# Weight totals of a seven-product matrix multiplication: prepared in DRAM for three FFN stages, with three products and the first tiles reordered

## The chip, the cores and the metric

The kernel runs on one core of a Trainium2 chip, in one launch. The metric is the device time of that launch in microseconds (us). Before the change it took 2440.33 us (median of three runs, 2434.14 to 2443.38). One further execution was recorded by the hardware profiler. The engines are named as in its profile: PE (TensorE, the matrix engine), PEld (its weight loads), DVE (VectorE), ACT (ScalarE), POOL (GpSimd) and SP (the engine whose queue issues most DMAs).

## The reference, cut to what matters

```python
def reference(x, ...):                    # x: (1, 512, 1024), two layers
    for l in range(2):
        h = rms_norm(x, norm_g[l, 0])
        x = x + 0.5 * swiglu(h, ffn_w_gate[l, 0], ffn_w_up[l, 0], ffn_w_down[l, 0])
        ...                               # three attention branches, gates, W_o: the "mixer"
        h = rms_norm(x, norm_g[l, 2])
        x = x + 0.5 * swiglu(h, ffn_w_gate[l, 1], ffn_w_up[l, 1], ffn_w_down[l, 1])
    return rms_norm(x, final_g)

def swiglu(h, w_gate, w_up, w_down):      # 1024 x 2816, 1024 x 2816, 2816 x 1024
    return (jax.nn.silu(h @ w_gate) * (h @ w_up)) @ w_down
```

All is float32. The kernel gets that precision by splitting each operand into a high part (a cast) and a low part (the remainder), and adding high x high, high x low and low x high.

## The kernel before

The program is a chain of stages: FFN (0,0), mixer 0, FFN (0,1), FFN (1,0), mixer 1, FFN (1,1), with (layer, place) as the code counts them. An FFN has a gate-up part and a down part. The 2816 hidden features are 22 tiles of 128. The first two tiles of a gate-up part (four in stage (0,0)) are plain: 24 matmuls of 512 columns for the gate, 24 for the up half. Every later tile is done by `Seven.tile` (L535), which replaces eight block products by seven, with sums of blocks as operands. Stages (0,1), (1,0) and (1,1) are called ready stages, since a part of their weight sums lies prepared.

A tile's weights are four blocks of 128 x 512 side by side, two of the gate (A11, A12) and two of the up weight (A21, A22). A tile needs:
- `wa`: the gate tile as it is, for products 1 and 2. It is loaded to `raw` (L494).
- `w31`: the gate tile and the up tile added in a certain way, for products 5 and 7. It is `wsum`, loaded ready from the DRAM tile `d_s` in ready stages (L434); in stage (0,0) the sum is made by an accumulating DMA (L438).
- `w24`: two further totals, made in place in `raw` by `others` (L502) once `wa` has been parted: the first half of `raw` gets the second half of `wsum` added, then the second half gets the first half added. In ready stages two accumulating DMAs of POOL do that (L507). In stage (0,0), and for the first tile of every stage, two additions of DVE do it (L509). They serve products 6 and 3.
- `w22`: A22 alone, for product 4, loaded to `a22` (L500).

`parted` (L99) casts a tile to its high half on ACT (L102) and subtracts on DVE (L103). `raw` has three buffers, `wsum` two, the halves four.

The matmuls of a tile stand on PE in the order 1, 5, 4 of the tile before, 6, 2, 3, 7. Products 1, 6, 7 and 4 gather in one PSUM bank (`mm` in the rows), 5 and 3 in another (`pr`), 2 in a third (`pv`). Product 6 may start only when ACT has copied product 1 out of the shared bank (L580). Each product has four matmuls with the high half of the weights and then four with the low half. In ready stages products 2 to 7 are "wide": one matmul takes 512 columns, the high and the low half of the other operand at once. The low half of the weights meets 256 columns (L523). In stage (0,0) only products 3, 4 and 5 are wide.

`in_order` fixes the order of a tile's instructions on each engine to the order of the code; the engines are otherwise coupled by semaphores. In a tile, ACT and DVE do this, in order: sum of product 7, `wa` of the next tile (with the two POOL DMAs behind it), `w24` of this tile, the copies of products 1 and 5, `w22`, the copy of 6, and `w31` of the next tile. In the first tile `sides.last()` (L602) also makes the fourth operand side.

`prepare` (L441) is a generator whose steps make the `d_s` tiles: a step copies 512 KB from DRAM to DRAM on SP's queue (L454) and lets POOL add the up tile to an earlier copy (L449). `weights` (L82), which loads every plain weight tile, advances it, by a rate held in `owed`. This happens in the mixers alone: in mixer 0 for two stages, at 48 steps on 72 weight loads, and in mixer 1 for one, at 24 on 72.

`position_tables` and `small_values` (L213, L253) make small tables for the attention. They stand ahead of tile 8 of stage (0,0) (L297).

Of the kernel before, what the change touches and what calls it, by code (L numbers as in the profile page):

```python
# [16 lines left out]
P = 128  # L17
# [14 lines left out]
GBUFS = 2 * MF  # L32
WIDE, WIDE_FIRST = frozenset((2, 3, 4, 5, 6, 7)), frozenset((3, 4, 5))
# [3 lines left out]
def encoder(ctx: ExitStack, tc: tile.TileContext, a: dict, out: bass.AP):  # L37
# [42 lines left out]
    prepared, ahead, owed = {}, [], [0.0, 0.0]  # L80

    def weights(src, width=1024):  # L82
        raw = wpool.tile([P, 1024], F32, tag="raw", name="raw", bufs=3)
        hi = wpool.tile([P, 1024], F32R, tag="whi", name="whi")
        lo = wpool.tile([P, 1024], F32R, tag="wlo", name="wlo")
        for c in range(0, src.shape[-1], width):
            w = slice(c, min(c + width, src.shape[-1]))
            loaded[:] = [nc.sync.dma_start(raw[:, w], src[:, w]).ins]
            nc.scalar.copy(hi[:, w], raw[:, w])  # L89
            lower[:] = [nc.vector.tensor_tensor(out=lo[:, w], in0=raw[:, w], in1=f(hi[:, w]), op=ALU.subtract).ins]  # L90
        owed[0] += owed[1]
        while ahead and owed[0] >= 1:
            owed[0] -= 1
            with tc.issue_after(loaded[0]):
                if next(ahead[0], ahead) is ahead:
                    ahead.pop(0)
        return hi, lo
# [115 lines left out]
    def position_tables(fp):  # L213


        parts = fp.tile([64, 36], F32R, tag="g", name="parts", bufs=GBUFS)
        nc.scalar.copy(parts, tab)
        nc.vector.tensor_tensor(out=parts[32:64], in0=tab[32:64], in1=f(parts[32:64]), op=ALU.subtract)
        for i in range(2):
            ps = st_tile()  # L220
            nc.tensor.matmul(ps[0:36, :], parts, hot[i], start=True, stop=True)
# [60 lines left out]
    def ffn(l, i, h, nxt=None):  # L282

        with tc.tile_pool(name="ffn", bufs=1) as fp, ExitStack() as order:
# [3 lines left out]
            if first:  # L288
                xs, sides, ps = opening(l, i, h, fp, ghi, glo)
                order.enter_context(tc.issue_after(h.squared))  # L290
            else:
                sides = []
            loads = []
            start, plain = (2, 4) if first else (0, 2)
            for m in range(start, MF):
                if m >= plain:
                    if first and m == plain + 4:  # L297
                        with tiles.in_order():
                            position_tables(fp)
                            small_values(fp)  # L300
                    if m == plain:
# [124 lines left out]
    def added(l, i, m, fp, load=None):  # L426

        gu = a["w_gu"][l, i, m]
        with ExitStack() as order:
# [3 lines left out]
            if (l, i) in prepared:  # L433
                loaded[:] = [nc.sync.dma_start(t, prepared[l, i][m]).ins]  # L434
                return t.rearrange("p n c -> p (n c)")
# [5 lines left out]
    def prepare(l, i):  # L441


        prepared[l, i] = {}
        waiting = []

        def accumulate():
            t, src = waiting.pop(0)
            nc.gpsimd.dma_start(t.rearrange("p n c -> p (n c)"), src, accum_op=ALU.add, max_dma_last_dim=4096)  # L449

        for m in range(2, MF):
            gu = a["w_gu"][l, i, m]
            t = prepared[l, i][m] = dram.tile([P, 2, S], F32, tag=f"d_s{l}{i}_{m}", name="d_s")
            nc.sync.dma_start(t, gu.rearrange("n p c -> p n c")[:, :, 0:S])  # L454
            waiting.append((t, gu[1]))
            if len(waiting) > 2:
                accumulate()
            yield
        while waiting:
            accumulate()  # L460
            yield

    class Seven:


        def __init__(self, l, i, h, fp, sides, ghi, glo):
# [3 lines left out]
            self.raw, self.sums, self.a22, self.wa, self.w31 = {}, {}, {}, {}, {}  # L470
# [16 lines left out]
        def fetch(self, m, sums=None):  # L487

            if m >= MF:
                return  # L490
            (l, i), fp = self.at, self.fp
            self.sums[m] = sums or added(l, i, m, fp)
            self.raw[m] = wpool.tile([P, 1024], F32, tag="raw", name="raw", bufs=3)
            nc.sync.dma_start(self.raw[m], a["w_gu"][l, i, m, 0])  # L494
# [7 lines left out]
        def others(self, m, engine):  # L502

            s2, s4 = self.raw[m][:, :S], self.raw[m][:, S:]
            for out, more in ((s2, self.sums[m][:, S:]), (s4, s2)):
                if engine is nc.gpsimd:
                    engine.dma_start(out, more, accum_op=ALU.add)  # L507
                else:
                    engine.tensor_tensor(out=out, in0=more, in1=out, op=ALU.add)  # L509

        def product(self, n, bank, w, b, start=False, stop=False):


            (wh, wl), ps = w, bank[:, 0]
            for k, bk in enumerate(b):
                go = start and k == 0
                if n in self.wide:
                    nc.tensor.matmul(bank, wh[k], bk, start=go, stop=False, skip_group_check=True)  # L518
                else:
                    nc.tensor.matmul(ps, wh[k], bk[:, 0], start=go, stop=False, skip_group_check=True)  # L520
                    nc.tensor.matmul(ps, wh[k], bk[:, 1], start=False, stop=False, skip_group_check=True)  # L521
            for k, bk in enumerate(b):
                nc.tensor.matmul(ps, wl[k], bk[:, 0], start=False, stop=stop and k == 3, skip_group_check=True)  # L523
# [11 lines left out]
        def tile(self, m):  # L535
# [29 lines left out]
            with self.in_order():  # L565
                self.fetch(m + 2)
                self.fetch_a22(m + 1)
                self.product(1, one, blocks(wa), [s.b11 for s in sides], start=True)
                rest()
                if not last:  # L570
                    self.wa[m + 1] = room()
                    parted(self.raw[m + 1], self.wa[m + 1])
                    if self.ready:
                        self.others(m + 1, nc.gpsimd)
                if first:
                    self.others(m, nc.vector)
                parted(self.raw.pop(m), w24)
# [22 lines left out]
                if first:  # L600
                    for s in sides:
                        s.last()  # L602
                if not last and not self.ready:
                    self.others(m + 1, nc.vector)
# [12 lines left out]
                self.product(7, one, blocks(w31), side(3))  # L617
            u3 = self.halves(1, 6, 7)
# [706 lines left out]
    h = Norm(0, gain(0, 0))  # L1325
    for l in range(DEPTH):
# [103 lines left out]
```

## Time and profile before

| | |
|---|---|
| time, median of 3 runs | 2440.33 us (2434.14 to 2443.38) |
| profiled execution, its own time | 2435.98 us |
| its span | 2433.8 us, so 2.2 us lie around it |
| gate-up part with seven products, one tile in the steady state | 9.86 us |
| DMA traffic | 388.37 MB, mean 160 GB/s |
| DVE / ACT / POOL busy | 1713.3 / 1323.3 / 362.4 us |

How to read it: a busy engine is one that executes an instruction. The matmuls are pipelined and their ends are modelled, so what PE loses is read from its idle time and from the distance of the starts. An entry such as "[2.79 <-ACT gu L580]" says that the engine was idle for 2.79 us ahead of the row and that the end of ACT's instruction at L580 released it. "PEclk" is the share of the clock that TensorE was granted.

### The profile page before, as it was taken

The page shows a single profiled execution, that of the slowest core. Times are in us where ns is not written, and L with a number is a line of the kernel's source. Part 1 is how long each engine was busy: PE and PEld are TensorE (multiplying, and loading weights), DVE is VectorE, ACT ScalarE, POOL GpSimd, SP SyncE. Part 2 cuts the span into 40 slices and gives each one's busy share as a digit, 9 for nine tenths or more (in the row PEclk, how much of TensorE's full clock was granted, in tenths as well). Part 3 has the DMA queues.
Part 4 walks back from the last instruction along what each step waited for, and adds up shares of the span by engine and source line. Part 5 has one row for each costly group of instructions (what it writes and reads, how often), then busy time and mean ns, then how long its engine had stood idle before and what let it go on. Part 6 is the DMA issues. An engine that isn't in the chain of part 4 may idle for free.

```text
span 2433.8 us, 34871 instructions
## 1 busy us (share of the span) xinstructions
PE 2401.1 (99%) x12762; PEld 2056.0 (84%) x12762; DVE 1713.3 (70%) x3067; ACT 1323.3 (54%) x2433; POOL 362.4 (15%) x518
## 2 busy tenths in 40 slices
PE   9999999999999999999999999999999999999998
PEld 7899888888888888888888888888888888888887
DVE  7899345766666689993499983467666666998822
ACT  6566225756566456663256652367566564565631
POOL 3100013322100111110011110133110000111100
PEclk9999999999999999999999999999999999999999
DMA  6566368774776346664356654566544433565632
GB/s 198 155 188 176 122 183 229 201 198 124 200 185 182 132 137 184 186 176 135 113 155 185 184 158 131 165 185 154 151 132 130 141 112 123 160 183 156 182 121 69
DMA packets 138347, 388.37 MB, mean 160 GB/s; under 512 B 16248, under 2 KB 21672, under 8 KB 138176
## 3 DMA queue, kind: packets, MB, share of 16 engines
q1 hardware_dynamic: 97536, 278.50, 34.2%
q0 software_dynamic: 39488, 105.79, 21.7%
q8 instruction: 100, 1.64, 0.3%
q10 hardware_dynamic: 1152, 1.86, 0.2%
q14 instruction: 71, 0.58, 0.1%
HBM read 334.15 MB, written 75.53 MB: 168 GB/s over the span
## 4 chain that ended last, share of the span: by engine, by line
PE 92%; DVE 2%; DMA 2%; ACT 2%; issue 1%; POOL 0%; SPq 0%; POOLq 0%; ACTq 0%; DVEq 0%
PE mm L117 8%; PE mm L116 8%; PE mm L119 8%; PE mm L518 7%; PE mm L523 6%; PE pr L518 6%; PE mm L364 5%; PE mm L363 5%; PE mm L366 5%; PE pr L523 3%; PE pv L518 2%; PE mm L520 2%; PE mm L521 2%; PE mm L1214 2%; PE mm L1210 2%; PE mm L1209 2%
## 5 line engine op out<-in xcount | busy, mean ns | idle before, releaser
L89 ACT CAST whi<-raw 128x1024 fp32r<-128x1024 f32 (+1 forms) x258 | 265.6, 1032 | 401.8 <-PE mm L364 185.0
L90 DVE TENSOR_TENSOR wlo<-raw,whi 128x1024 fp32r<-128x1024 f32 (+1 forms) x258 | 313.7, 1216 | 227.8 <-ACT whi L89 108.5
L116 PE MATMUL mm<-h,whi 128*128 128x512 f32 x800 | 318.4, 398 | 0.0
L117 PE MATMUL mm<-h,whi 128*128 128x512 f32 x800 | 313.7, 392 | 0.0
L364 PE MATMUL mm<-g,whi 128*128 128x512 f32 x528 | 205.5, 389 | 0.0
L363 PE MATMUL mm<-g,whi 128*128 128x512 f32 x528 | 205.5, 389 | 0.0
L119 PE MATMUL mm<-h,wlo 128*128 128x512 f32 x800 | 197.7, 389 | 0.0
L103 DVE TENSOR_TENSOR wlo<-raw,whi 128x1024 fp32r<-128x1024 f32 x156 | 184.9, 1219 | 15.3 <-ACT whi L102 15.1
L119 PEld LDWEIGHTS mm<-h,wlo 128*128 128x128 f32 x800 | 150.2, 188 | 31.3
L102 ACT CAST whi<-raw 128x1024 fp32r<-128x1024 f32 x156 | 158.2, 1052 | 32.5 <-DMA raw<-raw 14.5
L117 PEld LDWEIGHTS mm<-h,whi 128*128 128x128 f32 x800 | 150.5, 188 | 29.0 <-DVE h L148 0.5
L116 PEld LDWEIGHTS mm<-h,whi 128*128 128x128 f32 x800 | 150.4, 188 | 29.0 <-ACT h L147 0.6
L366 PE MATMUL mm<-g,wlo 128*128 128x512 f32 x528 | 131.4, 389 | 0.0
L955 ACT ACTIVATE lg<-lg,negm 128x256 f32<-128x256 f32 (+1 forms) x192 | 114.2, 595 | 26.8 <-DVE negm L952 25.5
L625 ACT COPY gu<-mm 128x512 f32<-128x512 f32 (+1 forms) x78 | 42.0, 538 | 159.1 <-PE mm L523 154.6
L449 POOL DMA_DIRECT2D d_s<-in_w_gu x60 | 51.4, 857 | 474.3 <-DMA d_s<-in_w_gu 415.5
L366 PEld LDWEIGHTS mm<-g,wlo 128*128 128x128 f32 x528 | 99.1, 188 | 20.6
L363 PEld LDWEIGHTS mm<-g,whi 128*128 128x128 f32 x528 | 99.2, 188 | 20.4
L364 PEld LDWEIGHTS mm<-g,whi 128*128 128x128 f32 x528 | 99.1, 188 | 20.4
L556 DVE TENSOR_TENSOR gu<-pr,gu 128x256 f32<-128x256 f32 x234 | 98.1, 419 | 3.6 <-ACT gu L586 1.1
L507 POOL DMA_DIRECT2D raw<-wsum x57 | 49.7, 872 | 322.3 <-DVE wlo L103 289.6
L103 DVE TENSOR_TENSOR wlo<-wsum,whi 128x1024 fp32r<-128x1024 f32 x78 | 94.7, 1215 | 0.0
(326 smaller groups left out, 6011.5 us busy)
## 6 DMA issues: line engine op xcount, KB each, us to landing
raw<-in_w_gu SPq DMA_DIRECT2D x94, 512.0 KB, 4.5
d_s<-in_w_gu SPq DMA_DIRECT2D x60, 512.0 KB, 5.4
d_s<-in_w_gu POOLq DMA_DIRECT2D x60, 512.0 KB, 6.5
wsum<-d_s SPq DMA_DIRECT2D x60, 512.0 KB, 3.6
raw<-in_w_down SPq DMA_DIRECT2D x48, 512.0 KB, 3.6
raw<-in_w_gate SPq DMA_DIRECT2D x48, 512.0 KB, 4.2
raw<-in_w_qk SPq DMA_DIRECT2D x44, 512.0 KB, 3.8
a<-in_w_gu SPq DMA_DIRECT2D x78, 256.0 KB, 4.7
```

The source lines that it names most:

```text
L89: nc.scalar.copy(hi[:, w], raw[:, w])
L90: lower[:] = [nc.vector.tensor_tensor(out=lo[:, w], in0=raw[:, w], in1=f(hi[:, w]), op=ALU.subtract).ins]
L102: nc.scalar.copy(hi, src)
L103: nc.vector.tensor_tensor(out=lo, in0=src, in1=f(hi), op=ALU.subtract)
L116: nc.tensor.matmul(ps, wh, xhi[k], start=k == 0, stop=False)
L117: nc.tensor.matmul(ps, wh, xlo[k], start=False, stop=False)
L119: nc.tensor.matmul(ps, wl, xhi[k], start=False, stop=k == n - 1)
L363: nc.tensor.matmul(ps, w[k][0], ghi[c + k], start=c + k == 0, stop=False)
L364: nc.tensor.matmul(ps, w[k][0], glo[c + k], start=False, stop=False)
L366: nc.tensor.matmul(ps, w[k][1], ghi[c + k], start=False, stop=c + k == MF - 1)
L518: nc.tensor.matmul(bank, wh[k], bk, start=go, stop=False, skip_group_check=True)
L523: nc.tensor.matmul(ps, wl[k], bk[:, 0], start=False, stop=stop and k == 3, skip_group_check=True)
```

## The change

Four things change.

1. `prepare` makes two DRAM tiles for each weight tile: `d_odd` (what `d_s` was) and `d_even` (the two `w24` totals). One step holds two copies on SP's queue and up to three accumulating DMAs on POOL, each two steps behind the one that it needs. The steps are spread over more stages by the table `PACE`: the down parts of (0,0), (0,1) and (1,0), both mixers, and the seven-product tiles of (0,1). `drained` runs what is left when a stage begins.
2. In ready stages `d_even` is loaded to a `raw` buffer of its own, and neither POOL's two DMAs nor, in the first tile, DVE's two additions are there any more. SP's order is now `a22`, `wsum`, `raw`, `even`.
3. In the first tile of each stage, `wa` of the next tile is parted after the copy of product 6 rather than ahead of `w24`. The tables of stage (0,0) are cut in two: the operands and the small values stand ahead of tile 8, the matmuls and what follows them ahead of tile 9.
4. In products 2, 4 and 7 the four matmuls with the low half of the weights come first.

```diff
+PACE = {"mixer": (0.36, 0.3), "seven": {(0, 1): 0.4}, "down": {(0, 0): 0.3, (0, 1): 0.4, (1, 0): 0.25}}
+LOW_FIRST = (2, 4, 7)
...
-        owed[0] += owed[1]
-        while ahead and owed[0] >= 1:
...
+        ahead_by(owed[1])
...
         nc.vector.tensor_tensor(out=parts[32:64], in0=tab[32:64], in1=f(parts[32:64]), op=ALU.subtract)
+        yield
         for i in range(2):
...
+            drained(l, i)
+            owed[1] = 0
...
                     if first and m == plain + 4:
+                        tables = position_tables(fp)
                         with tiles.in_order():
-                            position_tables(fp)
+                            next(tables)
                             small_values(fp)
+                    if first and m == plain + 5:
+                        with tiles.in_order():
+                            list(tables)
...
+            owed[1] = PACE["down"].get((l, i), 0)
             for m in range(KC):
...
+        for k in range(2, MF + 6):
+            if k < MF:
...
+                tiles[k] = t31, t24
+                nc.sync.dma_start(t31, gu.rearrange("n p c -> p n c")[:, :, 0:S])
+                nc.sync.dma_start(flat(t24), gu[0])
+            if k - 2 in tiles:
+                accumulate(flat(tiles[k - 2][0]), a["w_gu"][l, i, k - 2, 1])
+            if k - 4 in tiles:
+                t31, t24 = tiles[k - 4]
+                accumulate(t24[:, 0], t31[:, 1])
+            if k - 6 in tiles:
+                t24 = tiles[k - 6][1]
+                accumulate(t24[:, 1], t24[:, 0])
             yield
...
+    def ahead_by(n):
+
+        owed[0] += n
+        while ahead and owed[0] >= 1:
+            owed[0] -= 1
+            with tc.issue_after(loaded[0]):
+                if next(ahead[0], ahead) is ahead:
...
+    def drained(l, i):
+
+        while (l, i) in due:
+            if next(ahead[0], ahead) is ahead:
...
+            self.raw[m] = raw(a["w_gu"][l, i, m, 0])
+            if self.ready:
+                self.even[m] = raw(prepared[l, i][m][1].rearrange("p n c -> p (n c)"))
...
-                if engine is nc.gpsimd:
-                    engine.dma_start(out, more, accum_op=ALU.add)
-                else:
-                    engine.tensor_tensor(out=out, in0=more, in1=out, op=ALU.add)
+                nc.vector.tensor_tensor(out=out, in0=more, in1=out, op=ALU.add)
+            self.even[m] = self.raw[m]
...
+            if n in LOW_FIRST:
+                low(False)
+                high(True)
+            else:
+                high(False)
+                low(True)
...
+            with self.in_order():
+                self.fetch_a22(m + 1)
+                self.fetch(m + 2)
+                self.product(1, one, blocks(wa), [s.b11 for s in sides], start=True)
+                rest()
+                if not first:
+                    next_wa()
+                elif not self.ready:
+                    self.others(m)
+                parted(self.even.pop(m), w24)
...
                 if first:
+                    next_wa()
                     for s in sides:
                         s.last()
...
+            ahead_by(PACE["seven"].get(self.at, 0))
...
+    due[:] = [(0, 1), (1, 0), (1, 1)]
+    ahead[:] = [prepare(*at) for at in due]
     for l in range(DEPTH):
...
-        ahead[:] = [prepare(*at) for at in ([(0, 1), (1, 0)] if l == 0 else [(1, 1)])]
-        owed[:] = 0.0, 24 * len(ahead) / 72
+        owed[1] = PACE["mixer"][l]
         mixer(l, n1, n2)
-        for steps in ahead:
-            for _ in steps:
-                pass
-        ahead.clear()
+        owed[1] = 0
```

What this moves on the engines is shown at three places. The first is DVE at the end of the plain tiles and in the first seven-product tile of stage (0,1). `wlo<-wsum` is the low half of `w31`, `wlo<-raw` of `wa` or `w24`, L384 and L128 finish the plain tile. Before:

```order
L103 TENSOR_TENSOR wlo<-wsum,whi 128x1024
L103 TENSOR_TENSOR wlo<-raw,whi 128x1024
L384 TENSOR_TENSOR gu<-pg,gu 128x512
L384 TENSOR_TENSOR gu<-mm,gu 128x512
L509 TENSOR_TENSOR raw<-wsum,raw 128x512
L128 TENSOR_TENSOR g<-gu,g 128x512
L509 TENSOR_TENSOR raw<-raw 128x512
L128 TENSOR_TENSOR g<-gu,g 128x512
L103 TENSOR_TENSOR wlo<-raw,whi 128x1024
L556 TENSOR_TENSOR gu<-pr,gu 128x256
L593 TENSOR_TENSOR w22l<-a_8861,w22h 128x512
L556 TENSOR_TENSOR gu<-gu 128x256
```

The same place with the change:

```order
L100 TENSOR_TENSOR wlo<-wsum,whi 128x1024
L100 TENSOR_TENSOR wlo<-raw,whi 128x1024
L389 TENSOR_TENSOR gu<-pg,gu 128x512
L389 TENSOR_TENSOR gu<-mm,gu 128x512
L125 TENSOR_TENSOR g<-gu,g 128x512 x2
L607 TENSOR_TENSOR gu<-pr,gu 128x256
L647 TENSOR_TENSOR w22l<-a_8913,w22h 128x512
L607 TENSOR_TENSOR gu<-gu 128x256
L100 TENSOR_TENSOR wlo<-raw,whi 128x1024
```

The two additions (L509) are gone, the early `wlo<-raw` is now `w24` of this tile, and the late one, now last, is `wa` of the next tile.

The second place is SP's queue in the seven-product tiles of stage (0,1), two tiles' worth. `a` is `a22`. Before:

```order
L434 DMA wsum<-d_s 128x1024
L494 DMA raw<-in_w_gu 128x1024
L500 DMA a_8983<-in_w_gu 128x512
L434 DMA wsum<-d_s 128x1024
L494 DMA raw<-in_w_gu 128x1024
L500 DMA a_9092<-in_w_gu 128x512
```

With the change:

```order
L439 DMA wsum<-d_odd 128x1024
L526 DMA raw<-in_w_gu 128x1024
L526 DMA raw<-d_even 128x1024
L538 DMA a_9147<-in_w_gu 128x512
L439 DMA wsum<-d_odd 128x1024
L465 DMA d_odd<-in_w_gu 256x1x512
L466 DMA d_even<-in_w_gu 16x8192
L526 DMA raw<-in_w_gu 128x1024
L526 DMA raw<-d_even 128x1024
L538 DMA a_9263<-in_w_gu 128x512
```

A tile loads `d_even` as well, and in eight of the twenty tiles of this stage the two copies of a step stand between the load of `wsum` and that of `raw`.

The third place is PE in a ready stage, products 2 and 3. Before:

```order
L518 MATMUL pv<-h_8497,whi 128x512
L518 MATMUL pv<-h_8539,whi 128x512
L518 MATMUL pv<-h_8581,whi 128x512
L518 MATMUL pv<-h_8623,whi 128x512
L523 MATMUL pv<-h_8497,wlo 128x256
L523 MATMUL pv<-h_8539,wlo 128x256
L523 MATMUL pv<-h_8581,wlo 128x256
L523 MATMUL pv<-h_8623,wlo 128x256
L518 MATMUL pr<-h_8497,whi 128x512
L518 MATMUL pr<-h_8539,whi 128x512
```

With the change:

```order
L555 MATMUL pv<-h_8541,wlo 128x256
L555 MATMUL pv<-h_8589,wlo 128x256
L555 MATMUL pv<-h_8631,wlo 128x256
L555 MATMUL pv<-h_8673,wlo 128x256
L555 MATMUL pv<-h_8541,whi 128x512
L555 MATMUL pv<-h_8589,whi 128x512
L555 MATMUL pv<-h_8631,whi 128x512
L555 MATMUL pv<-h_8673,whi 128x512
L555 MATMUL pr<-h_8541,whi 128x512
L555 MATMUL pr<-h_8589,whi 128x512
```

The same matmuls are there; eight wide ones now stand in a row where four did, and likewise eight narrow ones.

More of the change, by code (lines that the diff above doesn't have):

```diff
@@ L469, in __init__ @@
             self.wide = WIDE if self.ready else WIDE_FIRST
-            self.raw, self.sums, self.a22, self.wa, self.w31 = {}, {}, {}, {}, {}
+            self.raw, self.even, self.sums, self.a22, self.wa, self.w31 = {}, {}, {}, {}, {}, {}
             self.tail, self.behind = (), {}
@@ L500, in fetch_a22, with others, mm, high @@
                 nc.sync.dma_start(self.a22[m], a["w_gu"][self.at + (m, 1)][:, S:])
-        def others(self, m, engine):
+        def others(self, m):
             s2, s4 = self.raw[m][:, :S], self.raw[m][:, S:]
             for out, more in ((s2, self.sums[m][:, S:]), (s4, s2)):
-                if engine is nc.gpsimd:
-                    engine.dma_start(out, more, accum_op=ALU.add)
-                else:
-                    engine.tensor_tensor(out=out, in0=more, in1=out, op=ALU.add)
+                nc.vector.tensor_tensor(out=out, in0=more, in1=out, op=ALU.add)
+            self.even[m] = self.raw[m]
         def product(self, n, bank, w, b, start=False, stop=False):
[L514 to L523, printed above, removed]
+            (wh, wl), ps, count = w, bank[:, 0], [0]
+            def mm(out, wk, bk, last):
+                count[0] += 1
+                go, end = start and count[0] == 1, stop and last
+                nc.tensor.matmul(out, wk, bk, start=go, stop=end, skip_group_check=True)
+            def high(end):
+                for k, bk in enumerate(b):
+                    if n in self.wide:
+                        mm(bank, wh[k], bk, end and k == 3)
+                    else:
+                        mm(ps, wh[k], bk[:, 0], False)
+                        mm(ps, wh[k], bk[:, 1], end and k == 3)
+            def low(end):
+                for k, bk in enumerate(b):
+                    mm(ps, wl[k], bk[:, 0], end and k == 3)
+            if n in LOW_FIRST:
+                low(False)
+                high(True)
+            else:
+                high(False)
+                low(True)
         def halves(self, *n):
@@ L564, in tile, with next_wa @@
             w24 = room()
[L565 to L569, printed above, removed]
+            def next_wa():
                 if not last:
@@ L572, in tile @@
                     parted(self.raw[m + 1], self.wa[m + 1])
[L573 to L577, printed above, removed]
+            with self.in_order():
[8 more added lines that the diff above has]
+                parted(self.even.pop(m), w24)
                 rest()
```

43 lines of the change are left out of this document (20 added, 23 removed).

## The prediction

> **What bounds the kernel now.** First the page's busy times, then PE's waits, then the stages.
>
> ```profile
> span 2433.8 us, 34871 instructions
> PE 2401.1 (99%) x12762; PEld 2056.0 (84%) x12762; DVE 1713.3 (70%) x3067; ACT 1323.3 (54%) x2433; POOL 362.4 (15%) x518
> ...
> PE mm L518 <- ACT gu L580: 12.8, 8, 3.0
> PE mm L520 <- ACT gu L580: 2.4, 1, 2.4
> ```
>
> PE is busy for 2401.1 of 2433.8 us. The change takes no matmul away, so it can win only idle PE time and time at a lower clock. The waits view (engine and line, what it waited for, total us, count, longest) has one wait that matters: product 6 waits until ACT has copied product 1 (L580), 15.2 us in nine places. Windows by stage (length, busy times, then granted clock, DMA share, GB/s) show where:
>
> ```profile
> 364.00:832.00 468.00, 465.04 (x2404) 391.27 (x2403) 316.63 (x660) 285.93 (x599) 93.28 (x140) 1.00 0.68 182
> 876.00:1090.00 214.00, 210.98 (x1257) 186.52 (x1255) 202.97 (x352) 137.10 (x233) 34.87 (x40) 1.00 0.64 177
> 1566.00:2032.00 466.00, 464.78 (x2408) 391.96 (x2409) 311.98 (x661) 285.94 (x599) 84.58 (x122) 1.00 0.51 141
> 2090.00:2310.00 220.00, 213.16 (x1253) 188.26 (x1252) 198.86 (x337) 138.78 (x232) 34.24 (x40) 0.98 0.64 176
> ```
>
> The first and third are mixers 0 and 1, the others the gate-up parts of (0,1) and (1,1). In these DVE is nearly as full as PE (202.97 of 214), which matters below. A stall of PE costs more than itself. Narrow windows behind three stalls give the clock (before the last two numbers):
>
> ```profile
> 1244.20:1250.90 6.70, 5.79 (x18) 4.92 (x19) 4.18 (x9) 4.41 (x10) 0.87 (x1) 0.52 0.90 249
> 2210.20:2213.50 3.30, 3.30 (x12) 2.77 (x11) 2.66 (x6) 1.50 (x3) 0.87 (x1) 0.53 0.33 58
> 2234.10:2237.40 3.30, 3.30 (x12) 2.76 (x11) 2.63 (x6) 1.52 (x3) 0.87 (x1) 0.53 0.28 49
> ```
>
> Half the clock for 6.7, 3.3 and 3.3 us loses 3.4 + 1.7 + 1.7 = 6.8 us. The Trainium skill, TensorE: Matmul & The Clock Gate, section "Why this matters for your kernels", says that gaps up to about 3 us are safe. Here idle times of 2.42 to 2.96 us (rows below) stand right ahead of the drops, so by this trace they belong to the stalls; by the rule they would not, which is rival C.
>
> **The totals loaded instead of added by POOL.** In the steady state of a ready stage the rows are these (start, length, engine):
>
> ```profile
> 1344.66 2.35 DVE L103 TENSOR_TENSOR wlo<-raw,whi 128x1024 fp32r<-128x1024 f32 x2
> 1346.28 0.86 POOL L507 DMA_DIRECT2D raw<-wsum  x1 [5.24 <-DVE wlo L103]
> 1350.57 0.89 POOL L507 DMA_DIRECT2D raw<-raw  x1 [3.42 <-DMA raw<-wsum]
> 1353.23 2.00 ACT L102 CAST whi<-raw 128x1024 fp32r<-128x1024 f32 x2
> 1355.66 0.36 ACT L580 COPY gu<-mm 128x256 f32<-128x256 f32 x1
> 1356.79 1.09 PE L518 MATMUL mm<-pair,whi 128*128 128x512 f32 x4
> ...
> DMA to landing us min/median/max: 3.2/3.4/6.1
> ...
> DMA to landing us min/median/max: 4.1/4.5/7.1
> ```
>
> The subtraction of the next `wa` (the first of the two at 1344.66) releases POOL, whose two DMAs run one behind the other, at 3.4 us median each (of the landing rows the first is L507's, the second that of L494's loads of `raw`). The second lands at 1350.57 + 3.4 = 1354.0, and ACT's second cast (1353.23 + 1.0) needs it at 1354.2. Slack 0.2 us, and 0.8 more until product 6, which starts 1356.79 - 1356.02 behind the copy. A landing of 6.1 breaks that, as here in stage (1,1):
>
> ```profile
> 2201.63 0.86 POOL L507 DMA_DIRECT2D raw<-raw  x1 [4.63 <-DMA raw<-wsum]
> 2207.70 1.04 ACT L102 CAST whi<-raw 128x1024 fp32r<-128x1024 f32 x1 [3.58 <-DMA raw<-raw]
> 2209.59 1.42 PE L518 MATMUL mm<-pair,whi 128*128 128x512 f32 x4 [2.79 <-ACT gu L580]
> 2233.50 1.45 PE L518 MATMUL mm<-pair,whi 128*128 128x512 f32 x4 [2.42 <-ACT gu L580]
> ```
>
> With the change `raw` of tile m+2 takes the buffer of `even` of tile m. Its load waits for the end of the pair of subtractions (1344.66 + 2.35 = 1347.0), lands 4.5 later at 1351.5, and is cast at 1353.2: slack 1.7 plus 0.8, with one DMA in place of two. `even` itself has a whole tile more. So the mid-stage stalls should go. Their sum is 12.8 us less the three at first tiles (5.4, below), 7.4, and two of the clock windows, 3.4: **-10.8**.
>
> What one copy of a step takes, by the page's list of issues (size, median us to landing):
>
> ```profile
> d_s<-in_w_gu SPq DMA_DIRECT2D x60, 512.0 KB, 5.4
> ```
>
> Stage (0,1) pays for it, since eight steps of preparation run in its tiles. Mixer 0 has 24 more steps than mixer 1 and a DMA share of 0.68 against 0.51; 0.17 x 467 us / 24 = 3.3 us of all DMA engines for an old step, and about 6.6 for a new one, which moves twice as much. At 0.4 steps a tile the share there goes from 0.64 towards 0.9 (0.4 x 6.6 / 9.86 = 0.27, with 9.86 us a tile). The copies stand ahead of `raw` on SP's queue. No row shows a step beside such a tile: by the median landing it costs nothing, by the longest `raw` landing in the rows, 7.1, it is 7.1 - 4.5 - 2.5 = 0.1 late, and should both copies (5.4 for one) queue ahead of it, some 3 us. I take 0.25 us for each of the eight, **+2**, nearer to the first two, with 0 and +38 (rival A) as ends.
>
> **The first tile of the ready stages.** Stage (1,0), with what PE and ACT waited for:
>
> ```profile
> 1241.52 0.63 PE L523 MATMUL pr<-pair,wlo 128*128 128x256 f32 x4
> 1242.98 0.68 DVE L509 TENSOR_TENSOR raw<-raw 128x512 f32<-128x512 f32 x1
> 1243.75 1.04 ACT L102 CAST whi<-raw 128x1024 fp32r<-128x1024 f32 x1 [2.97 <-DVE raw L509]
> 1245.12 2.08 PE L518 MATMUL mm<-pair,whi 128*128 128x512 f32 x4 [2.96 <-ACT gu L580]
> ...
> 899.17 1.20 PE L518 MATMUL mm<-pair,whi 128*128 128x512 f32 x4 [1.23 <-ACT gu L580]
> ```
>
> DVE's additions (L509) hold ACT's cast of `w24`, which holds the copy of product 1. With `even` loaded and parted early, product 6 can start when product 5 ends. That removes 2.96, 1.23 in (0,1) and about as much in (1,1), 5.4 together, and the clock window of 3.4. What is late next is DVE: `wa` of tile 3 is now subtracted behind `w22` and the copy of 6, and the four subtractions of `sides.last()` come behind it. I count on in DVE's new order from 1241.2 (three instructions of 512 columns, 0.6 each, ahead of the row at 1242.98), with 1.13 for a subtraction of 1024 columns (half of 2.35, less the overlap), 0.6 for 512, 0.4 for 256, and ACT's casts where they come later. DVE then ends `w24` of the second tile at about 1254.0. That tile starts at 1241.5 + 0.5 + 4 x 1.4 = 1247.6 and its product 6 needs the low half 5.2 later (4.3 for products 1, 5 and 4, 0.9 for its high half), at 1252.8. So a new wait of about 1.2 us in each of three stages; a wait of that size did not lower the clock at 899 (four wide matmuls in 1.20, against 2.08 at 1245). Together -5.4 - 3.4 + 3.6 = **-5.2**; the ends are -8.8 with no new wait, and -2 with one of 2.3.
>
> **The tables in (0,0).**
>
> ```profile
> 91.19 0.64 PE L523 MATMUL mm<-side,wlo 128*128 128x256 f32 x4
> 93.81 0.83 PE L221 MATMUL st<-hot,parts 64*36 64x512 f32 x2 [1.97 <-DVE parts L218]
> 96.02 0.18 DVE L257 TENSOR_SCALAR bg<-bg 128x24 f32<-128x24 f32 x1
> 98.29 0.20 ACT L265 ACTIVATE ls<-ls 128x2 f32<-128x2 f32 x1 [1.21 <-DVE ls L264]
> 102.50 0.35 ACT L580 COPY gu<-mm 128x256 f32<-128x256 f32 x1
> 102.90 0.39 PE L520 MATMUL mm<-pair,whi 128*128 128x256 f32 x1 [2.44 <-ACT gu L580]
> ```
>
> PE's own wait (1.97) goes, but ACT is what is late: the second exponential (98.29) waits for a DVE chain (from L257 on), ahead of which the table work takes 2.2 us (from the operands' end at 93.8 to 96.0). That moves behind, so the copy and product 6 come about 2.3 earlier; PE, being earlier by more, waits longer there (about 4.6). The table matmuls (0.8) move to the next tile. Net -1.5, less a longer clock window after the longer wait: **-1**, with -3 and +3 as ends.
>
> **The mixers.** Mixer 0 idles PE for 468 - 465.0 = 3.0 us, mixer 1, at half the steps, for 466 - 464.8 = 1.2; POOL's accumulations wait for copies, and the attention's POOL work waits behind them. At 0.36 steps a load mixer 0 becomes like mixer 1: **-1.5**, with -3 and +2 as ends, since a step now has three POOL DMAs. Mixer 1 keeps its rate (0.3 against 0.33). In the down parts three buffers are loaded ahead, each worth 24 matmuls of 0.227 (1.81 / 8, below), 5.4 us; that covers a copy's 5.4, and if it did not, each of some 23 steps there could cost up to 1 us.
>
> **Low halves first.** It makes eight wide and eight narrow matmuls stand in a row. The rows for product 7 (four wide, four narrow) and for product 1 (twelve narrow):
>
> ```profile
> 1341.28 1.09 PE L518 MATMUL mm<-side,whi 128*128 128x512 f32 x4
> 1342.21 0.64 PE L523 MATMUL mm<-side,wlo 128*128 128x256 f32 x4
> 1342.68 0.28 PE L520 MATMUL mm<-h,whi 128*128 128x256 f32 x1
> ...
> 1343.64 0.64 PE L523 MATMUL mm<-h,wlo 128*128 128x256 f32 x4
> ...
> 243.52 1.81 PE mm L366 x8
> ```
>
> By the starts four wide take 0.93 us and four narrow 0.47. In the down part (last row, of the chain of waits) eight wide ones take 1.81, so 0.905 for four; with four of six wide groups joined that end is -0.025 x 4 x 60 tiles = -6. In the long narrow row of product 1 eight take 0.96, so 0.48 for four; that end is +0.01 x 6 x 60 = +3.6. I take **0**, by the rows of the same groups.
>
> **Sum.** -10.8 + 2 - 5.2 - 1 - 1.5 = -16.5 from the profiled execution's own 2436.0 (2433.8 and 2.2 around it): 2419.5. The median of the runs before is 4.3 above that execution, and the irregular stalls are what differs between runs; since they go, I give **2420** for the changed kernel.
>
> **Rivals.** *A, slower:* in stage (0,1) the copies and accumulations starve `raw`. For it: share 0.9, and the copies ahead of `raw`. Against: `raw` has 2.5 us of slack. It decides from landings above 7.0. If a step makes it 10, each of eight steps stalls 3 us and the clock drop adds 1.7: 8 x 4.7 = 38 in place of 2, so 2456. The Trainium skill, DMA: Bandwidth & Descriptors, section "Issuing engines are not separate DMA queues", speaks for it: DMAs of all queues run on the same 16 engines and interleave. The rows bear that out in part, since L507's landing reaches 6.1 over a median of 3.4. *B, no change to measure:* the stalls come back by another DMA. `raw`'s chain also runs through DVE, whose lag in the second tile delays the load; if five waits of this size remain, 10.8 is lost and the time is 2431. *C:* the half clock is not the stalls' doing and comes in any case; then 6.8 stay, 2427. The clock-gate page's rule would have it so. *D:* no new wait in the second tiles and no cost in (0,1): 2414. That the order does not change as told is excluded by the rows shown ahead.
>
> **How the numbers follow.** Forecast 0.62 (2410 to 2430), A 0.10, B 0.18, C 0.05, D 0.05. The range leaves out A and a tail below: 2407 to 2438. A measurement of this kernel tells about 0.5% from no change, so faster means below 2428, slower above 2452.5. Faster: most of the forecast (0.58), C and D, 0.68. Same: B and the rest, 0.22. Slower: A, 0.10.
>
> **What would show it.** No wait of ACT on a DMA in stages (1,0) and (1,1), and none at the first product 6; a wait of about 1 us at product 6 of the second tile, released by DVE; no half clock after 1240; L526 of `raw` landing under 7 us in (0,1); product groups of 0.93 and 0.47. Repeated waits of product 6 in (0,1) would make it wrong, and so would four wide matmuls that take another time in their new neighbourhood.

## The result, and the profile after

The changed kernel takes 2518.74 us (median of four runs, 2516.38 to 2522.49), against 2441.14 us of the kernel before on the same chip (four runs, 2434.14 to 2443.38). The ratio is 1.0324, with a 95% interval of 1.0299 to 1.0349: slower by 78 us, where the forecast was 2420.

The head of the page of the changed kernel (busy time, share of the span, instructions):

```profile
span 2514.5 us, 34878 instructions
...
PE 2413.9 (96%) x12762; PEld 2063.4 (82%) x12762; DVE 1722.1 (68%) x3061; ACT 1328.3 (53%) x2433; POOL 349.0 (14%) x524
```

PE idled 33 us before (2433.8 - 2401.1) and idles 101 now. Its busy time also grew, by 13 us with the same 12762 matmuls, so it ran longer at a low clock (the clock of the two mixer stretches stands in the windows view below). PE's waits in the changed kernel (engine and line, what it waited for, total us, count, longest):

```profile
PE st L184 <- POOL rs L177: 25.1, 2, 16.8
PE t L1042 <- POOL lg L1109: 23.6, 5, 8.6
PE st L184 <- POOL rt L177: 11.4, 2, 9.5
PE mm L368 <- ACT whi L91: 7.5, 2, 4.6
PE mm L555 <- ACT gu L634: 7.1, 7, 4.0
```

The wait for ACT's copy of product 1 (L634 now) has halved, from 15.2 to 7.1 us. Three waits of 60 us together are released by small pieces of POOL's work: a norm's scale (`rs`, `rt`) and the clearing of a logits tile (`lg`). The kernel before had only one of them, `lg`, with 1.4 us. The traces cut by stage show where. Each stretch below goes from the start of one matmul to the start of another; a stretch with a mixer goes from the last matmul of a down part to the first product 5 of the next gate-up part.

| stretch (us) | before | changed | accumulations apart |
|---|---|---|---|
| gate-up (0,0) | 184.9 | 185.0 | 184.8 |
| with mixer 0 | 535.8 | 580.6 | 536.8 |
| gate-up (0,1) | 198.1 | 201.4 | 195.5 |
| down (0,1) | 121.0 | 132.9 | 121.1 |
| gate-up (1,0) | 200.6 | 195.4 | 195.5 |
| with mixer 1 | 533.0 | 568.9 | 532.6 |
| gate-up (1,1) | 205.3 | 194.9 | 194.9 |

The last column is the first experiment. The rest (the other down parts, the norm, the finish) agrees within 0.4 us. The two stretches with a mixer lose 44.8 + 35.9 = 80.7 us, which is the whole difference of the spans (2514.5 - 2433.8 = 80.7); the other rows cancel. The gate-up parts of (1,0) and (1,1) won 15.6.

Those two mixer stretches in the windows view of the changed kernel (length, busy times, then granted clock, DMA share, GB/s):

```profile
360.80:941.40 580.60, 539.77 (x2714) 452.11 (x2713) 372.80 (x735) 316.19 (x642) 108.37 (x168) 0.97 0.58 161
1617.30:2186.10 568.80, 539.26 (x2713) 451.89 (x2712) 364.49 (x737) 316.24 (x642) 101.57 (x157) 0.98 0.54 149
```

The DMA engines are busy for 0.58 and 0.54 of the time, so they are not full. The timeline of POOL at the start of mixer 0 (start, length, engine, instruction, in brackets the idle time ahead and its releaser), with DVE's row that makes the scale's input `rt` ahead of it and the matmul of PE that waited behind it:

```profile
369.93 0.15 DVE L176 TENSOR_SCALAR rt<-st 128x4 f32<-128x4 f32 x1
372.97 0.86 POOL L456 DMA_DIRECT2D d_even<-d_odd  x1 [9.21 <-DMA d_odd<-in_w_gu]
...
381.12 0.82 POOL L456 DMA_DIRECT2D d_even<-d_even  x1 [7.29 <-DMA d_even<-d_odd]
381.65 1.12 POOL L456 DMA_DIRECT2D d_odd<-in_w_gu  x1
382.20 1.16 POOL L67 DMA_DIRECT2D d_x<-x  x1
389.19 0.86 POOL L456 DMA_DIRECT2D d_even<-d_odd  x1 [5.83 <-issue]
389.75 1.37 POOL L177 TENSOR_TENSOR rs<-rt,nhalf 128x4 f32<-128x4 f32 x1
391.18 1.12 PE L184 MATMUL st<-ident,rs 128*128 128x128 f32 x4 [16.79 <-POOL rs L177]
```

The scale `rs` is work of 1.37 us. Its input is ready at 370.1, but it starts at 389.75, since it stands in POOL's queue behind accumulations. POOL stops at each of them until the one before has landed: 9.21 us, then 7.29, then 5.83. (For the third the profile names no releaser; the accumulation ahead of it, issued at 381.65, landed at 388.6.) PE stands for 16.79. In the code each accumulation is two steps behind the one that it needs. The compiled order of POOL does not keep that distance. These are its rows for two tiles (numbers at the names tell the tiles apart):

```
L456 DMA d_odd_2874<-in_w_gu 128x1024
L456 DMA d_even_2875<-d_odd_2874 128x512
L456 DMA d_even_2875<-d_even_2875 128x512
L456 DMA d_odd_2975<-in_w_gu 128x1024
L456 DMA d_even_2976<-d_odd_2975 128x512
L456 DMA d_even_2976<-d_even_2976 128x512
```

All three accumulations of one tile follow each other, and each reads what the one ahead of it writes. The Trainium skill, DMA: Bandwidth & Descriptors, section "Two DMAs through the same engine are not ordered", has the issuing engine wait for the first of two such transfers before it issues the second; the brackets above agree. So the waits cannot go, only the distance can grow. What that costs POOL, in its own waits (the changed kernel, then the kernel before):

```profile
POOL d_even L456 <- DMA d_odd<-in_w_gu: 342.5, 51, 12.7
POOL d_odd L456 <- DMA d_odd<-in_w_gu: 274.9, 28, 58.7
POOL d_even L456 <- DMA d_even<-d_odd: 233.7, 53, 8.1
```

```profile
POOL d_s L449 <- DMA d_s<-in_w_gu: 415.5, 48, 20.1
```

Before, POOL waited 415.5 us for 60 tiles, 6.9 us a tile (8.7 for each of the 48 waits); now it waits 851 us, 14.2 a tile, in up to three waits.

### The profile page after: what moved, and what is told of

Its sections match the earlier page's. It is cut to its first block, busy times and chain, and to the rows that moved or that the text cites. A ratio compares the mean times of both kernels' runs of the same rounds, so it can differ in the third digit from the quotient of the medians.

```text
span 2514.5 us, 34878 instructions
## 1 busy us (share of the span) xinstructions
PE 2413.9 (96%) x12762; PEld 2063.4 (82%) x12762; DVE 1722.1 (68%) x3061; ACT 1328.3 (53%) x2433; POOL 349.0 (14%) x524
## 5 line engine op out<-in xcount | busy, mean ns | idle before, releaser
L92 DVE TENSOR_TENSOR wlo<-raw,whi 128x1024 fp32r<-128x1024 f32 (+1 forms) x258 | 321.2, 1246 | 214.5 <-ACT whi L91 120.2
L456 POOL DMA_DIRECT2D d_even<-d_odd x60 | 50.4, 840 | 381.9 <-DMA d_odd<-in_w_gu 342.5
L1253 DVE TENSOR_TENSOR z<-mm,rb 128x512 f32<-128x512 f32 x48 | 33.2, 691 | 97.4 <-PE mm L116 97.4
L892 DVE SCALAR_TENSOR_TENSOR qn<-mm,rb 128x512 f32<-128x512 f32 x44 | 34.8, 795 | 94.7 <-PE mm L116 68.6
```

## The experiments

Two theories were set against each other. **W**: POOL stands in waits because each accumulation is issued right behind the one that it needs, and the attention's POOL work stands behind it. **T**: the doubled traffic holds up the loads.

**The accumulations really two steps apart.** Each accumulation is put, in issue order alone, behind the accumulation ahead of it in the program and behind the last copy of two steps later. Copies and bytes stay the same.

```
-            nc.gpsimd.dma_start(out, more, accum_op=ALU.add, max_dma_last_dim=4 * 1024)
+            add = nc.gpsimd.dma_start(out, more, accum_op=ALU.add, max_dma_last_dim=4 * 1024).ins
+            for one in behind:
+                why = mybir.DependencyInfo(mybir.DependencyClass.NoSync, mybir.DependencyReason.DATA)
+                tc.add_manual_dep(add, one.name, why, reason="lag")
+            behind[1:] = [add]
...
-                nc.sync.dma_start(flat(t24), gu[0])
+                behind[:1] = [nc.sync.dma_start(flat(t24), gu[0]).ins]
```

> The changed kernel, with the three accumulations of a step kept two steps apart in POOL's order (issue order only, no wait added; the same copies, the same bytes). Measured by the stretch from the last matmul of a down part to the first product 5 of the next gate-up part: 535.8 and 533.0 us in the kernel before, 580.6 and 568.8 in the changed one. Theory W (POOL stands in waits, because each accumulation is issued right behind the one that it needs, and the attention's POOL work stands behind it): both stretches come back to within 6 us of the kernel before, and the time to about 2519 - 40 - 32 = 2447, or down to 2430 if the stalls of stage (0,1) and of its down part (7 and 12 us) go as well. Theory T (the doubled traffic holds up the loads): the stretches stay above 565 and the time above 2500.

Measured: 2417.07 us (2415.46 to 2419.1), a ratio to the kernel before of 0.9901 (0.9876 to 0.9926). POOL's timeline in mixer 0 now, and the windows of the two stretches:

```profile
379.45 0.85 POOL L456 DMA_DIRECT2D d_odd<-in_w_gu  x1
380.08 1.07 POOL L456 DMA_DIRECT2D d_even<-d_odd  x1
380.61 1.38 POOL L456 DMA_DIRECT2D d_even<-d_even  x1
```

```profile
361.00:897.80 536.80, 532.44 (x2713) 447.47 (x2712) 360.58 (x735) 315.92 (x641) 118.68 (x173) 1.00 0.64 177
1558.30:2090.90 532.60, 531.63 (x2717) 447.73 (x2716) 358.76 (x738) 316.76 (x644) 117.50 (x164) 1.00 0.58 162
```

The three are issued within 1.2 us of each other and wait for nothing, since they now belong to three different tiles. Both stretches are back at the length of before, the clock at 1.00, while the DMA share is higher than in the slow kernel (0.64 against 0.58). POOL's waits for the steps' transfers fell from 851 to 222 us. Its busy time in mixer 0 did not fall (118.68 us against 108.37 in the slow kernel), so it was not POOL's own work that cost the time, but its standing still. That is theory W, and T cannot give it. The 12 us of down (0,1) and the 6 of gate-up (0,1) came back too.

**The traffic alone**, added to the kernel before:

```
             nc.sync.dma_start(t, gu.rearrange("n p c -> p n c")[:, :, 0:S])
+            spare = dram.tile([P, 2, S], F32, tag=f"d_even{l}{i}_{m}", name="d_even")
+            nc.sync.dma_start(spare.rearrange("p n c -> p (n c)"), gu[0])
```

> The kernel before, with one more copy of 512 KB a step on SP's queue into a buffer in DRAM that nobody reads: the traffic of the new copies without their accumulations. Mixer 0 then carries 40 of them, mixer 1 20. Theory W: the two stretches stay within 4 us of 535.8 and 533.0, the time within 0.5% of 2441. Theory T: at the 44.8 us that 26 steps cost in the changed kernel's mixer 0, 40 copies cost at least 20 us there and some 10 in mixer 1; time above 2465.

Measured: 2443.01 us, a ratio of 1.0007 (0.9985 to 1.0029). Mixer 1 takes 532.6, as W has it. Mixer 0 takes 545.4, 9.6 more, which neither theory gave; there the DMA share is 0.72, and PE's waits name POOL again:

```profile
PE t L988 <- POOL lg L1055: 3.8, 1, 3.8
...
PE st L187 <- POOL rs L180: 2.4, 1, 2.4
```

So traffic costs something where 40 copies stand in one mixer, and half of the 9.6 us shows as a longer wait behind POOL (6.2 us here, 1.4 in the kernel before). In the whole time it is not to be measured; in this execution gate-up (1,1) took some 10 us less than in the kernel before.

**The waits alone**, added to the kernel before, behind its accumulation:

```
+            s1, s2 = [dram.tile([8, 64], F32, tag=f"d_spare{n}", name="d_spare", bufs=2) for n in "ab"]
+            nc.gpsimd.dma_start(s1, t[0:8, 1, 0:64])
+            nc.gpsimd.dma_start(s2, s1)
```

> The kernel before, with two small copies of 2 KB on POOL's queue behind each accumulation, the first reading what the accumulation wrote, the second what the first wrote: the chain of waits on POOL without the traffic. Theory W: mixer 0 longer by 20 to 60 us, mixer 1 by 10 to 30, PE's waits there released by POOL; time 2470 to 2530. Theory T: 2 KB are nothing, the stretches stay within 4 us, the time within 0.5% of 2441.

Measured: 2472.99 us in one run. Mixer 0 takes 562.8, 27.0 more; mixer 1 538.0, only 5.0 more, under the 10 to 30 expected. The waits of PE from 360 to 900 us:

```profile
PE t L989 <- POOL lg L1056: 14.0, 2, 11.5
PE st L187 <- POOL rs L180: 4.3, 1, 4.3
```

Some 4 KB a step make mixer 0 longer by 27 us, and PE's waits name the same POOL work as in the changed kernel. In mixer 1 they give 5 of the 35.9 us only, so there the case rests on the first experiment.

**Which of the waits.** The accumulations apart from each other, but the first of them free to stand right behind its own copy (shown against the version of the first experiment):

```
-            behind[1:] = [add]
+            behind[:] = [add]
...
-                behind[:1] = [nc.sync.dma_start(flat(t24), gu[0]).ins]
+                nc.sync.dma_start(flat(t24), gu[0])
```

> The changed kernel with the accumulations in the order of the code (two steps apart from each other), but the first one not held behind the copies of two steps later: it may again stand right behind its own copy. Theory W asks which of the waits it was. If the chain between the accumulations is all, the stretches with the mixers are 537 and 533 us as with both, and the time 2415 to 2422. If the wait for the copy counts as much (it is 8 us a step in the kernel before, which bears it), the stretches are 5 to 20 us longer, time 2425 to 2450.

Measured: 2425.77 us in one run; 538.9 and 540.4 us. POOL's wait and PE's:

```profile
POOL d_odd L456 <- DMA d_odd<-in_w_gu: 535.0, 49, 59.6
```

```profile
PE t L1047 <- POOL lg L1114: 7.7, 4, 3.2
```

Single waits of 10.9 us (535.0 / 49) cost 2 and 8 us in the two stretches, counted from the version with the accumulations apart. The chain of three cost 44 and 36. The first wait counts, then, but most of the price is the chain between the accumulations.

**The kernel before, with its one accumulation held back in the same way:**

```
-            nc.gpsimd.dma_start(t.rearrange("p n c -> p (n c)"), src, accum_op=ALU.add, max_dma_last_dim=4096)
+            add = nc.gpsimd.dma_start(t.rearrange("p n c -> p (n c)"), src, accum_op=ALU.add, max_dma_last_dim=4096).ins
+            why = mybir.DependencyInfo(mybir.DependencyClass.NoSync, mybir.DependencyReason.DATA)
+            tc.add_manual_dep(add, behind[0].name, why, reason="lag")
...
-            nc.sync.dma_start(t, gu.rearrange("n p c -> p n c")[:, :, 0:S])
+            behind[:] = [nc.sync.dma_start(t, gu.rearrange("n p c -> p n c")[:, :, 0:S]).ins]
```

> The kernel before, with its one accumulation a step held behind the copy of two steps later. POOL waits there 415 us in 48 places. If such waits cost nothing as long as there is one a step, the stretches stay at 535.8 and 533.0 within 2 us and the time within 0.5% of 2441; if the gain of the version with the accumulations apart over the kernel before comes from the lag itself and not from the loaded totals, this one comes near it, below 2428.

Measured: 2433.39 us (2426.95 to 2445.86), a ratio of 0.9973 (0.9954 to 0.9992); 533.5 and 532.8 us. It gains 0.27% (0.08 to 0.46), so most of the 1% of the first experiment comes from the rest of the change, not from the distance alone. By the runs below the low halves give 3 us of that, the tables nothing, and the new order of the first tiles loses 6, which leaves the loaded totals; that is worked out, not tried alone.

**Low halves first, undone** in the changed kernel:

```
-LOW_FIRST = (2, 4, 7)
+LOW_FIRST = ()
```

> The changed kernel with the high halves first in all products (the list of products with low halves first is empty). A steady tile of a ready stage takes 9.86 us in the kernel before and 9.81 in the changed one. If that is the order of the halves, it is 9.86 again, 3 us in 60 tiles, less than a look can tell in the time (2519 to 2522); if it is the missing POOL accumulations, it stays at 9.81. Under neither theory do the mixers change: 580 and 569 us within 5.

Measured: 2527.95 us in one run. Product 2's wide group in two tiles that follow each other, first in this version, then in the changed kernel:

```profile
1337.30 1.09 PE L555 MATMUL pv<-h,whi 128*128 128x512 f32 x4
1347.16 1.09 PE L555 MATMUL pv<-h,whi 128*128 128x512 f32 x4
```

```profile
1316.28 1.09 PE L555 MATMUL pv<-h,whi 128*128 128x512 f32 x4
...
1326.10 1.09 PE L555 MATMUL pv<-h,whi 128*128 128x512 f32 x4
```

9.86 against 9.82 us (9.81 in most tiles): the new order is worth 0.05 us a tile, 3 us in 57 tiles. Mixer 0 took 589.0 here, 8.4 more than in the changed kernel and against the expectation, and down (0,1) took 5 more; the cause of both stays open.

**The first tiles in the order of before**, on the version with the accumulations apart:

```
-                if not first:
-                    next_wa()
-                elif not self.ready:
+                next_wa()
+                if first and not self.ready:
                     self.others(m)
...
                 if first:
-                    next_wa()
                     for s in sides:
```

> The changed kernel with the accumulations two steps apart (2417.07 us), and the first tiles in the order of before: the weights of the next tile are parted ahead of w24 in all four stages. The second term of the prediction put 5.2 us on the new order. Theory O (the order does it): product 6 of the first tile waits again 1 to 3 us in each ready stage, with half the clock behind the longest, against 1.7 us saved in each second tile (11.48 to 9.81 us): time 2417 to 2424. Theory E (the loaded total alone does it, since the two additions of DVE are gone, and the new order only moves a wait to the second tile): no wait over 1 us at the first product 6, second tiles at 9.81 and in (0,0) at 9.94, time 2410 to 2413.

Measured: 2411.55 us (2411.31 to 2411.79), a ratio of 0.9885 (0.9847 to 0.9924). The first two tiles of (1,0), first with the new order (from the changed kernel; with the accumulations apart the first tile is as long within 0.1 us), then with the old one:

```profile
1304.80 1.09 PE L555 MATMUL pv<-h,whi 128*128 128x512 f32 x4
...
1313.08 1.19 PE L555 MATMUL mm<-pair,whi 128*128 128x512 f32 x4 [0.16 <-ACT gu L634]
1315.22 0.74 PE L555 MATMUL mm<-pair,wlo 128*128 128x256 f32 x4 [0.96 <-DVE wlo L100]
...
1316.28 1.09 PE L555 MATMUL pv<-h,whi 128*128 128x512 f32 x4
```

```profile
1237.04 1.20 PE L560 MATMUL mm<-pair,whi 128*128 128x512 f32 x4 [0.21 <-ACT gu L638]
1239.02 1.09 PE L560 MATMUL pv<-h,whi 128*128 128x512 f32 x4
1248.84 1.09 PE L560 MATMUL pv<-h,whi 128*128 128x512 f32 x4
```

With the new order the second tile takes 11.48 us (1316.28 - 1304.80) and waits for DVE in product 6; with the old one it takes 9.82, and the first product 6 waits 0.21. The loaded total alone removes the wait of 2.96 us of before. The order only adds one, in (0,0) as well (11.68 against 9.94 us).

**The same two once more, side by side on one chip:**

> The changed kernel with the accumulations two steps apart, once more, beside the next one on one chip. The new order of the first tiles delays each second tile by 1.67 us in four stages, 6 to 7 us in all by the tiles, against 0.6 of a wait at the first product 6 that it takes away in stage (0,1): this one is to take about 5.5 us more than the next (0.2% of the time).

> The changed kernel with the accumulations two steps apart and the first tiles in the order of before, once more: about 5.5 us under the one beside it, 2411 to 2413, and a ratio to the kernel before of 0.988. If the 5.5 us seen between two earlier jobs were the chip's, the two agree within 1.5 us.

Measured: 2417.37 us (2415.13 to 2421.73) with a ratio of 0.9916 (0.9902 to 0.993), and 2411.24 us (2408.11 to 2412.71) with 0.9885 (0.9868 to 0.9902). The 6.1 us between them are the order of the first tiles. The second is the fastest version of this study.

**The position tables whole again**, on the version with the accumulations apart:

```
-                            next(tables)
+                            list(tables)
                             small_values(fp)
```

> The changed kernel with the accumulations two steps apart, and the position tables whole in one tile of (0,0), as before. The prediction put 1 us on the split. If that is so, tile 8 of (0,0) and the next, 15.15 and 11.79 us with the split, take 16 to 19 and 11 to 12 us, 1 to 3 more in sum, and PE waits about 2 us for the tables' operands again; if the split only moves the wait, the sum stays within 0.5 us of 26.9. In the time of one look neither is to be seen (2417 to 2420).

Measured: 2419.89 us in one run. PE's wait of 1.97 us for the tables' operands is back. From one product 2 to the next, tile 8 of (0,0) and the one behind it take 17.01 + 9.94 = 26.95 us, with the split 15.15 + 11.79 = 26.94. The split moves a wait and wins nothing.

## Why the prediction was wrong, step by step

- **The mixers: this step failed.** It took -1.5 us with -3 and +2 as ends; measured were +44.8 and +35.9. The prediction compared steps per weight load and DMA share, and named the cause in half a sentence ("a step now has three POOL DMAs") without pricing it. The row to price it from was there: one accumulation a step made POOL stand for 8.7 us at a time. The price of three depends on whether they wait for each other, and that stands in POOL's compiled order, where the three of one tile are neighbours; the description of the change took the distance from the code. Why they were compiled next to each other stays open. Keeping the distance removes the loss, and waits without traffic make 27 of the 44.8 us in mixer 0.
- **The down parts** were put at nothing, with up to 1 us a step. Down (0,1) lost 11.9. The waits from 1143 to 1290 us:

```profile
ACT h L144 <- DVE x L276: 64.2, 8, 23.0
POOL d_even L456 <- DMA d_odd<-in_w_gu: 52.3, 6, 12.7
...
DVE x L276 <- DMA x<-d_x: 41.8, 3, 20.2
```

```profile
1207.36 0.59 POOL L62 DMA_DIRECT2D x<-d_x  x1
1212.55 0.72 ACT L144 ACTIVATE h<-x,ng 128x512 fp32r<-128x512 f32 x1 [23.04 <-DVE x L276]
1214.78 0.79 PE L368 MATMUL mm<-g,whi 128*128 128x512 f32 x1 [4.64 <-ACT whi L91]
```

The step was priced by copies on SP's queue. What was late was `x`, whose transfers POOL also issues, behind its accumulations: again POOL's queue. DVE and then ACT wait for `x`, ACT's cast of the next weights stands behind that, and PE waits for the cast. With the accumulations apart the part takes 121.1.

- **Stage (0,1), rival A.** One tile stalled, not eight: `raw` of 954.16 was cast at 965.62, where ACT had waited for it, in 50 us of a DMA share of 0.99.

```profile
965.62 1.99 ACT L99 CAST whi<-raw 128x1024 fp32r<-128x1024 f32 x2 [4.74 <-DMA raw<-in_w_gu]
```

```profile
940.00:990.00 50.00, 44.91 (x260) 39.26 (x259) 40.95 (x71) 29.70 (x51) 9.04 (x11) 0.93 0.99 281
```

Rival A had the place and the mechanism, but not the size. What crowded there were accumulations left over from earlier steps: counted from the first product 5 of the stage, seven are issued within 18 us, against three with the accumulations apart. That this burst made the stall is argued from the two traces, not tried alone. In the version with them apart, the longest landing of `raw` from the weights is 7.75 us and of `even` 9.19, and no tile stalls for over 0.6 us but the second. The 7.75 let ACT wait 1.05 us for `raw` and made that tile 0.58 us longer, which fits the limit of 7.0 us that the prediction worked out.

- **The totals loaded (-10.8 with the clock): right.** In the waits of ACT for `raw` during gate-up (1,0) and (1,1), the kernel before has these rows, and the changed one has none:

```profile
ACT whi L102 <- DVE raw L509: 3.0, 1, 3.0
ACT whi L102 <- DMA raw<-raw: 2.4, 3, 1.3
```

```profile
ACT whi L102 <- DMA raw<-raw: 8.6, 4, 3.6
ACT whi L102 <- DVE raw L509: 1.2, 1, 1.2
```

- **The first tiles (-5.2):** the new wait, put at 1.2 us and released by DVE, came as the product 6 rows above show (0.96, and 1.67 for the whole tile). But the gain was credited to the order when the loaded total alone gives it, and (0,0), which pays 1.74, was left out. From (0,1), (1,0) and (1,1) together the version with the accumulations apart wins 2.6 + 5.1 + 10.4 = 18.1 us. The steps for these stages give 10.8 + 5.2 - 2 = 14.0, and 17 with the 3 us of the low halves.
- **Low halves first:** 0 was taken, -6 to +3.6 as ends; -3 measured, by the distance of the tiles.
- **The tables:** -1 was taken, -3 to +3 as ends; 0 measured.
- **The sum:** 2420 fits the kernel that the code describes (2417.07), and not the one that was compiled. Even there the fit is in part luck: the ready stages won 18.1 us rather than 14.0, while the mixers and the tables gave nothing rather than 2.5.

## What to carry to other kernels

A distance written in the code between a transfer and its reader is worth only what the compiled order keeps of it: look up the neighbours on the issuing queue and what each waits for, and tie them with an issue-order dependency if the compiled order closes the gap. When an in-order engine that also serves the critical path gets transfers with waits, price the time that it stands still per step, not its busy time (POOL was busy for 14% of the span). A total that is loaded ready-made can make a reordering done for it needless: test them apart.

## What the runs showed of the hardware

POOL's waits for the steps' transfers came to 598 us with the first accumulation free (535 of them in the row above), at a cost of 10 us in the two mixer stretches; to 614 us with the small chain, at a cost of 32; and to 851 us in the changed kernel, at a cost of 81. So the sum of the waits does not give the price: chains of waits cost more than single ones.

The clock again went with the idle time ahead, but not with its length alone. With the first accumulation free (first fence) PE waited 2.67 us and then ran at half the clock for 4.7; in the version with the accumulations apart (second fence) 2.52 us of waiting left it at full speed, though the prediction's rows have half the clock behind 2.42:

```profile
1630.07 0.90 PE L1047 MATMUL t<-ident,lg 128*128 128x128 f32 x3 [2.67 <-POOL lg L1114]
...
1630.90:1635.60 4.70, 4.70 (x13) 3.64 (x12) 1.35 (x3) 0.48 (x1) 2.20 (x5) 0.50 1.00 211
```

```profile
367.55 0.50 PE L113 MATMUL mm<-h,whi 128*128 128x512 f32 x1 [2.52 <-ACT h L144]
...
367.60:371.00 3.40, 3.40 (x18) 2.72 (x18) 1.52 (x3) 1.47 (x2) 1.03 (x2) 1.00 0.83 214
```

The Trainium skill, TensorE: Matmul & The Clock Gate, section "Why this matters for your kernels", draws the line at gaps of about 3 us; here 2.67 was too long. With the accumulations apart PE waits for none that long behind 110 us, and no stretch at half the clock is left between there and the finish, so rival C, by which the half clock comes in any case, falls.
